# A matmul with batch normalization: four output stores of the last column tile issued as two transfers each

## The chip, the cores and the metric

The kernel runs on one core of a Trainium2 chip. The metric is the device time of one execution in microseconds (us), median of three runs. Details are read from one further execution, taken with the hardware profiler.

## The reference

```python
x: (16, 512, 1024) float32, weight: (1024, 768) float32, gamma = 1, beta = 0, eps = 1e-5
y = np.matmul(x, weight)
mean = np.mean(y, axis=(0, 1), keepdims=True)
var = np.var(y, axis=(0, 1), keepdims=True)
y_norm = (y - mean) / np.sqrt(var + eps)
return (gamma * y_norm + beta).astype(np.float32)
```

Mean and variance are taken for each of the 768 columns over all 8192 rows, so no value of a column can be written before all rows of that column are multiplied.

## The kernel before, in words

The 8192 rows are C = 16 chunks of CH = 512 rows, the 768 columns NT = 6 tiles of P = 128. GpSimd's queue loads x and the weight from HBM and casts them to bf16 on the way; VectorE transposes x in blocks of 32, and TensorE multiplies. The first two column tiles are computed with rows on the partitions, the other four with columns on the partitions; these have to be turned back before they are stored. Statistics are gathered by VectorE, ScalarE and GpSimd beside the matmuls. A column tile is finished, normalized and stored while TensorE works on the next one. What is left at the end is the last column tile (nt = 5).

The functions do not emit instructions at once. Each makes a `task` with a due time, engines, dependencies and buffers, and `arrange` puts all tasks into one order from estimated durations. The tasks then emit in that order, and `seq` (line 293) chains every instruction to the one before it on its engine, so that each engine, SyncE (SP) with its store queue too, works strictly in the order planned.

The part around the change is the loop over `ends` (lines 1363 to 1396). It cuts the last column tile into eleven blocks of rows, in the order of their first chunk c: two of 256 rows, two of 512, six of 1024 (c = 3, 5, 7, 9, 11, 13) and one of 512 (c = 15). For each block:
- `norm_part` (line 1374, VectorE) scales and shifts the bf16 block `y_sb` with the final coefficients `fss`, which `affine` (line 1350) has made;
- `turn_block` (line 1069, TensorE) transposes it, 128 by 128 at a time, into a PSUM bank `o_ps`;
- `copy` (line 1387, ScalarE) copies the bank to the SBUF tile `o_sb` of 128 partitions, as float32;
- `store` (lines 1389 to 1392, SP's queue) writes it to the output `out_dram`. A partition holds `count` rows of 128 floats, 512 bytes each, that go to rows of the output which lie 128 rows apart. With 1024 rows in the block, a partition sends 8 pieces of 512 bytes, and the store carries 512 KB.

Stores ahead of these, from the ring buffer (lines 1208, 1228 and 1281), use the same queue of SP. The transfers of SP's queue take their completion semaphores in turn from a set of eight, so a transfer also waits for the landing of the eighth before it.

Of the kernel before, what the change touches and what calls it, by code (L numbers as in the profile page):

```python
# [227 lines left out]
def kernel(  # L228
# [9 lines left out]
    nc = tc.nc  # L238
# [9 lines left out]
    P = 128  # L248
# [27 lines left out]
    MODE = {2:'xact',3:'xact',4:('pe',)*8}  # L276
    MODE = {nt: m if isinstance(m, tuple) else (m,) * (C // GY) for nt, m in MODE.items()}
    RAW, RAWADD, RAWDUE = {2:(0,2),3:(0,),4:(0,2,4)}, {2:'POOL',3:'POOL',4:'POOL'}, {2:14.0,3:8.0,4:8.0}
    RING = 3 * CH // 32 * KQ // 2
    ENG = {"ACT": nc.scalar, "DVE": nc.vector, "POOL": nc.gpsimd, "SP": nc.sync}  # L280

    x_flat = x.flatten_outer_dims()
    out_flat = out.flatten_outer_dims()
# [9 lines left out]
    def seq(bi):  # L293

        ins = bi.ins
        prev = last.get(ins.engine)
        if prev is not None:
            tc.add_manual_dep(
                ins, prev,
                mybir.DependencyInfo(mybir.DependencyClass.NoSync, mybir.DependencyReason.DATA),  # L300
                reason="order",
            )
        last[ins.engine] = ins.name
        return bi
# [5 lines left out]
    ident = singles.tile([P, P], bf16)  # L310
    ring = singles.tile([P, RING], f32)
    w_sb = singles.tile([P, JW, 2, N], bf16)
# [42 lines left out]
    tasks, turns = [], {}  # L355
    banks, xts, ys, sqs, rings = Pool(8), Pool(XT), Pool(YB), Pool(SQ), Space(RING)

    def task(prio, engines, emit, deps=(), lock=False, **kw):
        t = Task(prio, engines, emit, deps, **kw)
        t.lock = lock  # L360
        tasks.append(t)
        return t

    def dve(occ):
        return {"DVE": (occ, occ + 0.09)}

    def act(occ):
        return {"ACT": (occ, occ + 0.11)}
# [81 lines left out]
    for kind, n, *n1 in order:  # L450
# [11 lines left out]
        m0 = n if kind == "p" else n * rows  # L462
        if m0 == M // 2:
            affine_loads = affine = task(t, {"SP": (5.0, 7.0)}, load_affine, [x_ready[m0 // CH - 3, 0, JW]])
        slot = Slot(rings, rows // 32 * KQ // 2)
# [9 lines left out]
        for i in range(rows // QR):  # L475
            c, q = divmod(m0 // QR + i, QPC)
# [9 lines left out]
        if rows % QR:  # L486
            t0 = rows // QR * QR // 32
            m1 = m0 + 32 * t0
            c, q = divmod(m1 // QR, QPC)
# [197 lines left out]
    def y_of(nt, c):  # L687
        return y_col.setdefault((nt, c // GY), Slot(ys))

    def y(nt, c, n=1):  # L690
        group = y_of(nt, c).y.rearrange("p g m -> p (g m)")
        return group[:, c % GY * CH:(c % GY + n) * CH]
# [259 lines left out]
    p0 = task(U, {"ACT": (0.6, 0.7), "DVE": (0.6, 0.7)}, keep_affine, dl, takes=[aff_slot])  # L952


    def rows_out(c, s0, s1, k):
        due = S + 5.0 + 0.62 * k
        n = s1 - s0
        slot = Slot(rings, n * NA)

        def norm(eng):  # L960
            slot.o = piece(slot).rearrange("p (s n) -> p s n", n=NA)
            seq(nc.vector.tensor_mul(  # L962
                slot.o, y_row[c].y[:, s0:s1], aff[0][:, None, :].to_broadcast([P, n, NA])))

        def add(eng):
            row = sum1[:, NA:2 * NA] if eng == "POOL" else aff[1]
            seq(ENG[eng].tensor_add(slot.o, slot.o, row[:, None, :].to_broadcast([P, n, NA])))  # L967

        def store(eng):
            m0 = c * CH  # L970
            seq(nc.sync.dma_start(
                out_flat[m0 + s0 * P:m0 + s1 * P, 0:NA].rearrange("(s p) n -> p s n", p=P), slot.o))

        keeps = [row_end[k][3] for k in row_end if k[0] == c]
        a = task(due, dve(0.3 * n), norm, [p0] + keeps, takes=[slot], uses=[y_row[c], aff_slot])
        b = task(due + 0.4, dve(0.3 * n) if k in ADDED else pool(0.59 * n), add, [a, p0] if k in ADDED else [a] + dl,
                 uses=[slot, aff_slot] if k in ADDED else [slot])
        task(due + 1.0, {"SP": (0.38, 0.4)}, store, [b], dma=n * NA * P * 4 / 1024 / 365.0 * 1.024,
             uses=[slot])
# [76 lines left out]
    def turn_block(prio, nt, m0, count, deps, uses):  # L1056

        bank = Slot(banks)
        todo = []

        def step():
            if not todo:
                o_ps = psum.tile([P, count, P], bf16, tag="b")
                bank.tile = o_ps
                for s in range(count):
                    c, i = divmod(m0 // P + s, RT)
                    todo.append((o_ps[:, s], y(nt, c)[:, i * P:(i + 1) * P]))
            dst, src = todo.pop(0)
            seq(nc.tensor.transpose(dst, src, ident))  # L1069

        def emit(eng):
            for _ in range(emit.task.count):
                step()

        emit.step = step
        t = task(prio, pe(0.0555 * count), emit, deps, takes=[bank], uses=uses)
        emit.task = t
        turns[t] = [count, count]
        return t, bank

    def ga_block(c, due):
# [36 lines left out]
        turns[t] = [RT * GA, RT * GA]  # L1118
        d = task(due, {"ACT": (0.905, 1.0), "DVE": (1.1, 1.2)}, copy, [t], takes=[slot], uses=[bank])
        task(due, {"SP": (0.38, 0.4)}, store, [d], dma=RT * NA * P * 4 / 1024 / 365.0 * 1.024, uses=[slot])  # L1120

    for c in range(RC, C):
# [69 lines left out]
    def raw_block(nt, c, due):  # L1192
        rslot, turned = raw[nt, c]
        bank, t, k, b_sb = raw_aff[nt]
        slot = Slot(rings, GY * RT * P)
        n = GY * RT

        def norm_raw(eng):
            slot.o = piece(slot).rearrange("p (s n) -> p s n", n=P)
            seq(nc.vector.tensor_mul(slot.o, rslot.r, bank.tile[:, None, 0:P].to_broadcast([P, n, P])))  # L1200

        def add_raw(eng):
            row = b_sb if eng == "POOL" else bank.tile[:, P:2 * P]
            seq(ENG[eng].tensor_add(slot.o, slot.o, row[:, None, :].to_broadcast([P, n, P])))  # L1204

        def store(eng):
            m0 = c * CH
            seq(nc.sync.dma_start(
                out_flat[m0:m0 + n * P, nt * P:(nt + 1) * P].rearrange("(s p) n -> p s n", p=P), slot.o))

        a = task(due, dve(1.18), norm_raw, [t, turned], takes=[slot], uses=[bank, rslot])
        on = RAWADD[nt]
        b = task(due + 0.4, dve(1.2) if on == "DVE" else pool(2.35), add_raw, [a, t if on == "DVE" else k],
                 uses=[slot] + ([bank] if on == "DVE" else []))
        task(due + 1.0, {"SP": (0.38, 0.4)}, store, [b], dma=n * P * P * 4 / 1024 * STORE * 1.024, uses=[slot])
# [103 lines left out]
    nt = NT - 1  # L1319
# [45 lines left out]
    for c, r0, rows in ends:  # L1365
        due = E + 2.0 + 0.6 * c
        n = max(rows // CH, 1)
        keeps = [col_end[nt, c + i][1] for i in range(n) if c + i < C - 1]
        keeps += [col_end[nt, C - 1, q][1] for q in range(len(PIECES))] if c + n == C else []
        norms = []  # L1370
        for i in range(n):
            def norm_part(eng, c=c + i, r0=r0, rows=min(rows, CH)):
                part = y(nt, c)[:, r0:r0 + rows]
                seq(nc.vector.tensor_scalar(  # L1374
                    part, part, fss[:, 0:1], fss[:, 1:2], op0=ALU.mult, op1=ALU.add))

            norms.append(task(due + 0.6 * i, dve(0.323 if rows >= CH else 0.26), norm_part, [af] + keeps,
                              uses=[y_of(nt, c + i)]))
        m0 = c * CH + r0
        count = rows // P  # L1380
        b, bank = turn_block(due + 0.6 * (n - 1), nt, m0, count, norms, [y_of(nt, c + i) for i in range(n)])
        slot = Slot(xts)

        def copy(eng, slot=slot, bank=bank, count=count):
            o_sb = xtpool.tile([P, count, P], f32, tag="xT")
            slot.o = o_sb
            seq(nc.scalar.copy(o_sb, bank.tile))  # L1387

        def store(eng, slot=slot, m0=m0, count=count):
            seq(nc.sync.dma_start(  # L1390
                out_flat[m0:m0 + count * P, nt * P:(nt + 1) * P].rearrange("(s p) n -> p s n", p=P),
                slot.o))

        d = task(due + 0.6 * (n - 1), act(0.05 + 0.107 * count), copy, [b], takes=[slot], uses=[bank])
        task(due + 0.6 * (n - 1), {"SP": (0.6, 0.6)}, store, [d], dma=count * P * P * 4 / 1024 * STORE * 1.024,
             uses=[slot])
# [41 lines left out]
```

## Time and profile before

| what | us |
|---|---|
| median of three runs | 207.98 (207.83 to 208.24) |
| the profiled execution, whole | 208.35 |
| its span, first to last instruction | 206.6 |
| TensorE busy in the span | 190.2 (92%) |
| VectorE, ScalarE, GpSimd busy | 161.5, 149.0, 121.5 |
| last copy into `o_sb` ends (line 1387) | 196.95 |
| last store of `o_sb` is issued (line 1390) | 200.5 |

The profile's page has the busy time of each engine, the span cut in 40 slices with the busy share in tenths, and the share and the GB/s of the 16 DMA engines. The chain of waits follows the work that ended last back in time. Windows give the same figures for stretches that one chooses. The DMA view lists the packets of each queue and the transfers by line, with their time from issue to landing. No view gives the number of the DMA engine that a packet ran on. SP's own instructions are not counted as busy; "SPq" marks what it issues. The DMA share can be above 1 because packets of one engine overlap.

### The profile page before, as it was taken

What the parts mean: (1) busy time and instruction counts of PE and PEld (TensorE: products, weight loads), DVE (VectorE), ACT (ScalarE), POOL (GpSimd) and SP (SyncE); (2) the same over time, 40 slices, a digit from 0 to 9 for tenths busy, and PEclk for the clock granted to TensorE, in tenths of its full rate; (3) what the DMA queues carried; (4) which work ended last, traced back from release to release, by engine and by line L of the source; (5) the groups of instructions that cost most, each with busy time, mean ns of one, the idle gap of its engine ahead of it and who ended that gap; (6) DMA issues with size and microseconds to landing.
All of it is one profiled execution on the core that took longest, in us unless ns stands there. A gap on an engine that the chain in (4) does not pass through costs nothing. (4 is left out here: it accounts for less than half of the span.)

```text
span 206.6 us, 3499 instructions
## 1 busy us (share of the span) xinstructions
PE 190.2 (92%) x1202; PEld 115.6 (56%) x1202; DVE 161.5 (78%) x255; ACT 149.0 (72%) x273; POOL 121.5 (59%) x143
## 2 busy tenths in 40 slices
PE   7999999999999999999999999999999999995700
PEld 3467555656588888776855444444444445463700
DVE  4031979989999899969989999879999995668500
ACT  2001461479989989999889968989997979758910
POOL 7776964786499989997202999466603302741000
PEclk9999999999999999999999999999999999999665
DMA  5999999999999999999498699998999998999996
GB/s 76 163 199 194 191 196 196 199 195 196 190 194 197 195 197 195 196 197 192 89 135 229 231 333 335 275 363 230 354 291 235 336 316 217 349 343 345 345 347 181
DMA packets 98562, 48.74 MB, mean 236 GB/s; under 512 B 24304, under 2 KB 98032, under 8 KB 98544
## 3 DMA queue, kind: packets, MB, share of 16 engines
q0 software_dynamic: 34624, 18.36, 64.7%
q1 hardware_dynamic: 63920, 30.16, 53.4%
q8 instruction: 9, 0.15, 0.3%
q14 instruction: 9, 0.07, 0.1%
HBM read 36.71 MB, written 25.17 MB: 300 GB/s over the span
## 5 line engine op out<-in xcount | busy, mean ns | idle before, releaser
L577 PEld LDWEIGHTS <-w_sb 128*128 128x128 bf16 x520 | 50.4, 97 | 58.2 <-issue 0.5
L577 PE MATMUL y_ps<-xT_sb,w_sb 128*128 128x512 bf16 (+1 forms) x272 | 59.5, 371 | 0.0
L577 PE MATMUL y_ps<-x_pl,w_sb 128*128 128x512 bf16 x248 | 57.1, 379 | 0.2 <-ACT y_sb L717 0.2
L405 POOL DMA_DIRECT2D ring<-in_x_dram x76 | 47.4, 627 | 11.4 <-DMA ring<-in_x_dram 4.0
L512 PE MATMUL y_ps<-w_sb,xT_sb 128*128 128x256 bf16 x448 | 50.6, 273 | 0.6 <-DMA ring<-in_x_dram 0.4
L512 PEld LDWEIGHTS <-xT_sb 128*128 128x128 bf16 x448 | 43.5, 98 | 8.3 <-DVE xT_sb L437 2.0
L437 DVE STREAM_TRANSPOSE xT_sb<-ring 128x1024 f32<-128x1024 f32 (+1 forms) x29 | 31.2, 1112 | 13.9 <-DMA ring<-in_x_dram 13.7
L967 POOL TENSOR_TENSOR ring<-ring,sum 128x1024 f32<-128x1024 f32 (+1 forms) x11 | 23.8, 2186 | 20.0 <-DVE ring L962 20.0
L713 DVE BATCH_NORM_STATS2 stats<-y_ps 128x6 f32<-128x512 f32 x46 | 30.0, 682 | 5.7 <-PE y_ps L577 5.7
L549 ACT COPY x_pl<-xT_sb 128x1024 bf16<-128x1024 bf16 x31 | 31.6, 1059 | 1.9 <-DVE xT_sb L437 1.7
L717 ACT CAST y_sb<-y_ps 128x512 bf16<-128x512 f32 x51 | 28.4, 593 | 4.8 <-DVE stats L713 3.1
L661 ACT ACTIVATE sq_sb<-y_ps 128x512 f32<-128x512 f32 x28 | 16.3, 609 | 17.5 <-PE y_ps L512 16.9
L668 POOL TENSOR_TENSOR sum<-sum,sq_sb 128x512 f32<-128x512 f32 x20 | 25.6, 1281 | 3.4 <-ACT sq_sb L661 2.8
L664 DVE TENSOR_TENSOR sum<-y_ps,sum 128x512 f32<-128x512 f32 x28 | 18.9, 675 | 6.3 <-ACT sq_sb L661 5.3
L674 ACT CAST y_sb<-y_ps 128x512 bf16<-128x512 f32 x28 | 16.2, 597 | 8.1 <-DVE sum L664 7.8
L1204 POOL TENSOR_TENSOR ring<-ring,sum 128x1024 f32<-128x1024 f32 x6 | 14.4, 2424 | 10.5 <-issue 7.5
L962 DVE TENSOR_TENSOR ring<-y_sb,a_ps 128x1024 f32<-128x1024 bf16 (+1 forms) x16 | 16.7, 1076 | 0.6 <-DMA out_dram<-ring 0.6
L1069 PE MATMUL o_ps<-ident,y_sb 128*128 128x128 bf16 x104 | 13.8, 248 | 2.5 <-DVE y_sb L1374 2.5
L430 DVE STREAM_TRANSPOSE xT_sb<-ring 128x2048 bf16<-128x2048 bf16 x6 | 13.5, 2289 | 0.3 <-DMA ring<-in_x_dram 0.2
L1258 ACT CAST ring<-ring 128x1024 f32<-128x1024 bf16 x13 | 13.4, 1051 | 0.0
L593 PE MATMUL idle_ps<-idle_sb 128*128 128x512 f32 x18 | 10.7, 753 | 1.5 <-DVE idle_sb L316 1.5
L1171 POOL COPY sum<-sum 32x64 f32<-32x64 f32 (+1 forms) x7 | 3.0, 433 | 15.3 <-ACT sum L1171 8.7
(105 smaller groups left out, 161.5 us busy)
## 6 DMA issues: line engine op xcount, KB each, us to landing
out_dram<-ring SPq DMA_DIRECT2D x37, 512.0 KB, 3.8
ring<-in_x_dram POOLq DMA_DIRECT2D x52, 256.0 KB, 8.8
out_dram<-o_sb SPq DMA_DIRECT2D x6, 512.0 KB, 6.0
ring<-in_x_dram POOLq DMA_DIRECT2D x16, 128.0 KB, 5.7
w_sb<-in_weight_dram POOLq DMA_DIRECT2D x8, 192.0 KB, 6.2
out_dram<-ring SPq DMA_DIRECT2D x6, 256.0 KB, 2.8
ring<-in_x_dram POOLq DMA_DIRECT2D x4, 192.0 KB, 7.7
out_dram<-o_sb SPq DMA_DIRECT2D x3, 256.0 KB, 4.2
```

The costliest lines, as they stand in the source:

```text
L405: bi = seq(nc.gpsimd.dma_start(x_bf[32 * i:32 * i + 32], src[:, :, KQ * i:KQ * (i + 1)]))
L437: seq(nc.vector.transpose(dst, src[:, :, jw0:jw1]))
L512: seq(nc.tensor.matmul(y_ps[:, s], x_of(c, jw, e, t * P, (t + 1) * P), w_sb[:, jw, e, 0:NA], start=(s == 0 and jw == 0 and e == 0), stop=( ...
L549: seq(nc.scalar.copy(dst, pairs) if eng == "ACT" else ENG[eng].tensor_copy(dst, pairs))
L577: seq(nc.tensor.matmul(y_ps, w_sb[:, jw, e, nt * P:(nt + 1) * P], moving(c, jw, e, q0 * QR, q1 * QR, parted), start=(jw == 0 and e == 0 an ...
L661: seq(nc.scalar.activation(sq_sb[:, 0:n], slot.tile[:, 0:n], AF.Square))
L664: seq(nc.vector.tensor_add(sum1, slot.tile[:, 0:n], sum1))
L668: seq(ENG[eng].tensor_add(acc, acc, state["sq"][:, 0:n]))
L713: seq(nc.vector.bn_stats(dst, slot.tile))
L717: seq(nc.scalar.copy(y(nt, c), slot.tile))
L962: seq(nc.vector.tensor_mul(slot.o, y_row[c].y[:, s0:s1], aff[0][:, None, :].to_broadcast([P, n, NA])))
L967: seq(ENG[eng].tensor_add(slot.o, slot.o, row[:, None, :].to_broadcast([P, n, NA])))
```

## The change

Four of the eleven stores of the last column tile, those of the blocks with c = 3, 5, 7 and 9, are issued as two transfers each: the first over the partitions below a cut, the second over the rest. The cuts are at 120, 126, 104 and 108 of 128 partitions. The second transfer follows the first directly on SP's queue. The other seven stores remain whole, as one transfer over 128 partitions. The estimated durations of the tasks are left as they were, and the order on PE, DVE, ACT and POOL is the same; SP issues four transfers more. The line of these issues is 1390 before and 1394 after.

```diff
     RAW, RAWADD, RAWDUE = {2:(0,2),3:(0,),4:(0,2,4)}, {2:'POOL',3:'POOL',4:'POOL'}, {2:14.0,3:8.0,4:8.0}
+    CUTS = {3: 120, 5: 126, 7: 104, 9: 108}
     RING = 3 * CH // 32 * KQ // 2
...
-        def store(eng, slot=slot, m0=m0, count=count):
-            seq(nc.sync.dma_start(
-                out_flat[m0:m0 + count * P, nt * P:(nt + 1) * P].rearrange("(s p) n -> p s n", p=P),
-                slot.o))
+        def store(eng, slot=slot, m0=m0, count=count, cut=CUTS.get(c, P)):
+            dst = out_flat[m0:m0 + count * P, nt * P:(nt + 1) * P].rearrange("(s p) n -> p s n", p=P)
+            for p0, p1 in ((0, cut), (cut, P)):
+                if p0 < p1:
+                    seq(nc.sync.dma_start(dst[p0:p1], slot.o[p0:p1]))
```

SP's queue at the end, as transfers of partitions x rows x 128 floats, after the change:

```
L1394 DMACopy out_dram<-o_sb 128x2x128 x2
L1394 DMACopy out_dram<-o_sb 128x4x128 x2
L1394 DMACopy out_dram<-o_sb 120x8x128
L1394 DMACopy out_dram<-o_sb 8x8x128
L1394 DMACopy out_dram<-o_sb 126x8x128
L1394 DMACopy out_dram<-o_sb 2x8x128
L1394 DMACopy out_dram<-o_sb 104x8x128
L1394 DMACopy out_dram<-o_sb 24x8x128
L1394 DMACopy out_dram<-o_sb 108x8x128
L1394 DMACopy out_dram<-o_sb 20x8x128
L1394 DMACopy out_dram<-o_sb 128x8x128 x2
L1394 DMACopy out_dram<-o_sb 128x4x128
```

## The prediction

> **What bounds the kernel now.** First the page's slices of the whole span, to see which resource is full at the end.
>
> ```profile
> PE   7999999999999999999999999999999999995700
> DVE  4031979989999899969989999879999995668500
> ACT  2001461479989989999889968989997979758910
> DMA  5999999999999999999498699998999998999996
> ```
>
> One digit is 5.2 us. In the last two slices PE, DVE and ACT are idle and the DMA row still reads 9 and 6: the kernel ends on stores. Second, the chain of waits, whose last pieces are these.
>
> ```profile
> 189.89 5.66 ACT o_sb L1387 x7
> 195.55 0.92 ACTq L1433
> 196.46 0.49 ACT o_sb L1387
> ```
>
> The last copy into o_sb ends at 196.95 us and the span at 206.6, so 9.6 us lie behind all computing. Third, the windows of the tail, which tell what those 9.6 us are made of (columns: window, its length, busy time of PE, PEld, DVE, ACT and POOL, PE clock, DMA share, GB/s).
>
> ```profile
> 199.00:203.00 4.00, 0.00 (x0) 0.00 (x0) 0.00 (x0) 0.00 (x0) 0.00 (x0) 0.50 1.15 347
> 203.50:204.00 0.50, 0.00 (x0) 0.00 (x0) 0.00 (x0) 0.00 (x0) 0.00 (x0) 0.50 1.06 317
> 204.00:204.20 0.20, 0.00 (x0) 0.00 (x0) 0.00 (x0) 0.00 (x0) 0.00 (x0) 0.50 0.31 92
> 204.20:204.40 0.20, 0.00 (x0) 0.00 (x0) 0.00 (x0) 0.00 (x0) 0.00 (x0) 0.50 0.20 59
> 204.40:204.70 0.30, 0.00 (x0) 0.00 (x0) 0.00 (x0) 0.00 (x0) 0.00 (x0) 0.50 0.11 32
> 204.70:205.10 0.40, 0.00 (x0) 0.00 (x0) 0.00 (x0) 0.00 (x0) 0.00 (x0) 0.50 0.07 22
> 205.40:206.60 1.20, 0.00 (x0) 0.00 (x0) 0.00 (x0) 0.00 (x0) 0.00 (x0) 0.50 0.00 0
> ```
>
> All 16 DMA engines together move 347 GB/s, so one moves 347/16 = 21.7. In 204.70:205.10 the rate is 22: a single engine is left, and alone it runs at the pace that it had beside fifteen others. The engines are therefore limited one by one, and bytes shifted between them cost and gain time one for one. By the same division 92 GB/s is about four engines, 59 two to three, 32 one and a half. Read that way, twelve engines end by about 204.05 us, two at about 204.3, one at about 204.55 and the last at about 205.3. Call them the on-time engines and the late ones (0.35, 0.35, 0.6 and 1.4 us behind the earliest, which end at 203.9). From 205.3 the closing takes 1.3 us.
>
> Where the lateness comes from is in the DMA view of two short windows, 180.3 to 181.5 and 185.6 to 186.2: among the store packets lies a packet of the instruction queues.
>
> ```profile
> q8 instruction: 1, 0.02, 5.0%
> q14 instruction: 1, 0.01, 3.2%
> ```
>
> 5.0% of 16 engines over 1.2 us is 0.96 us of one engine, 3.2% over 0.6 us is 0.31 us. Two more of the small kind lie in 178.9:179.5 and 186.8:187.4. Four fetches on four engines and four late engines: I take the one for the other (an estimate from these rows).
>
> **The unit of the sum.** A 512 KB store takes 524288 B / 347 GB/s = 1.51 us, in which each engine moves 8 partitions of 8 rows of 512 B. One partition more or less on an engine is 1.51/8 = 0.189 us.
>
> **What the change moves.** No engine's instructions move but SP's, which issues 15 transfers on line 1394 where it issued 11 on line 1390. Bytes, rows of 512 B and copies stay. What is open is on which engines the cut transfers run. The trace has only transfers of 128 or 32 partitions, both multiples of 16, each in equal shares on all 16 engines. So I bound it: at one end a cut transfer is still spread evenly by packets and nothing moves; at the other it keeps equal shares of whole partitions and runs on as many engines as divide its partition count, always the same first ones. The numbers chosen, 15x8, 14x9, 13x8 and 12x9, lie nearer to the second end, since equal whole shares are what every row shows, and I take it. [...]
>
> Per engine, in partitions, before 8 for each of the four stores, 32 in all; after:
> - 120 and 8: 8 each on engines 0 to 14, and 1 each on 0 to 7.
> - 126 and 2: 9 each on 0 to 13, and 1 each on 0 and 1.
> - 104 and 24: 8 each on 0 to 12, and 2 each on 0 to 11.
> - 108 and 20: 9 each on 0 to 11, and 2 each on 0 to 9.
>
> The sums are 40 for engines 0 and 1, 39 for 2 to 7, 38 for 8 and 9, 36 for 10 and 11, then 25, 17, 8 and 0 for 12 to 15. So twelve engines gain 4 to 8 partitions (0.76 to 1.51 us) and four lose 7, 15, 24 and 32 (1.3, 2.8, 4.5 and 6.0 us). The lateness to be cured is at most 1.4 us, and a balance of all 16 would need only 7 partitions off the latest; the cut takes far more than that off the four and puts it on the rest.
>
> **The sum.** An on-time engine of 0 or 1 ends at 203.9 to 204.05 plus 1.51, that is 205.4 to 205.55, already past the old end of 205.3. Four more completion packets on each engine (the DMA view of 188 to 203 us counts 208 packets under 512 B for 13 transfers, 16 each) cost at most a 512 B packet's time, 512/21.7 = 24 ns each, 0.1 us in all; I take 0.04. Late engines that are among the loaded ones end later: the one at 204.55, on 2 to 7, at 204.55 + 1.32 + 0.04 = 205.9; one at 204.3 there at 205.65. For which engines are late no view gives numbers. In the packet records the engines restart in one order after the idle time at 172 us, and the latest one is about the 14th in it, the others about the 2nd, 7th and 9th; if that is the order of their numbers, the latest is spared and the others are not. That is what I take: the end of the DMA goes from 205.3 to 205.9, 0.6 us later. The profiled execution took 208.35 us, 206.6 of span and 1.75 around it, and becomes 208.95; the median of the three runs is 207.98, so 208.6.
>
> **What is hidden.** SP spends 0.42 us on a store's issue when nothing holds it (shortest of the row) and 1.35 in the median.
>
> ```profile
> L1390 SPq DMA_DIRECT2D out_dram<-o_sb x11: 419/1348/1617, 189.8 to 200.5; - x11
> DMA to landing us min/median/max: 3.8/5.1/6.1
> ```
>
> Four more issues are 4 x 0.42 = 1.7 us of SP time, with only further stores queued behind them. They lie beside transfers that land 3.8 to 6.1 us after their issue, so the engines have that much queued; without this cover the end would move by up to 1.7 us. Each transfer also waits for the landing of the eighth before it. For the last store that is now the 126-partition transfer, landing about 41 x 0.189 = 7.7 us before the end, near 198.2, when an engine has some 7 us of work in front of the last store. The spared engines run dry meanwhile, but 20 partitions of the last three stores take them 3.8 us; they are done near 201.5.
>
> **The rivals.**
> - *The latest engine is among the loaded ones.* Then the end is 205.3 plus 0.76 to 1.55: 208.8 to 209.5. For it: four spared engines of sixteen hold a given one by chance one time in four. Against it: its place in the order of restart.
> - *All late engines are spared.* Then engines 0 and 1 set the end, 205.45 to 205.6: 208.1 to 208.3.
> - *It ends faster: the transfers on fewer engines do not always run on the same ones.* If the first engine moves on from transfer to transfer, the skipped shares fall on different engines and the added ones spread. The latest loses 8 partitions once (1.5 us) and no on-time engine takes more than 3 (0.57): the DMA ends near 204.7, which gives 207.4. It decides as soon as the latest is skipped and no on-time engine takes over 4 partitions more (204.05 + 0.76 = 204.8). For it: 0.35 to 1.4 us of lateness is there to be won, mean lateness only 0.2. Against it: nothing in the trace shows a moving start.
> - *The cut transfers run slower.* Engines of an uneven cut may meet at the same part of SBUF. The nearest row is the loads of 32 partitions each, 195 GB/s on the page's slices against 347 here, though those also read HBM at twice what they write. At that pace a store takes 2.69 us, and four lose up to 4.7; a third of it, 1.5, is as much as I would give: 209.5 to 211. [...]
> - *The cut moves nothing between engines.* Even spreading by packets leaves the end at 205.3 plus 0.04: 208.0.
>
> **How the numbers follow.** About 0.2%, or 0.42 us, is what a measurement of this kernel can tell from no change. Chances: forecast (208.2 to 208.9, likeliest 208.6) 0.36; latest engine loaded 0.19; all late ones spared 0.13; slower transfers 0.09; nothing moved 0.06; faster 0.17. Slower: 0.19, 0.09 and all but 0.05 of the forecast, 0.59. Same: 0.13, 0.06 and that 0.05, 0.24. Faster: 0.17. The range from 207.4 to 209.7 leaves out half of the faster case and most of the slower transfers, some 0.16.
>
> **What would show it.** In the windows of the tail after, the rate should leave 347 GB/s well before 203 us as the spared engines run out (15, 14, 13 and 12 engines at work are 325, 304, 282 and 260 GB/s), stay near 260 until about 205, and drop to two or three engines near 205.5. A rate that holds 347 to 203.5 says that nothing was moved; an end of DMA before 204.9 says that the faster rival holds; single-engine rates below 21.7 say that the transfers slow each other. The prediction is wrong at its root if engines 0 and 1 don't get 8 partitions more.

## The result, and the profile after

The changed kernel is slower: 211.23 us in the median of four runs (210.23 to 211.91) against 208.06 for the kernel before on the same chip; ratio 1.0149, 95% interval 1.0106 to 1.0192, that is 3.1 us more (2.2 to 4.0). The profiled execution took 211.42 us, with a span of 209.6. The forecast was 208.6, the range ended at 209.7.

Computing is over at the same moment as before. This is the end of the chain of waits, after:

```profile
190.06 5.66 ACT o_sb L1388 x7
195.72 0.92 ACTq L1435
196.63 0.49 ACT o_sb L1388
```

The last copy ends at 197.1 us, 0.2 later than before; the rest lies behind it, nearly all of it in the stores. The windows of the tail, after (columns as in the prediction: the last two are DMA share and GB/s):

```profile
192.00:194.00 2.00, 2.00 (x21) 2.00 (x20) 2.00 (x7) 2.00 (x4) 0.00 (x0) 0.50 1.15 344
196.00:198.00 2.00, 0.00 (x0) 0.00 (x0) 0.00 (x0) 1.12 (x2) 0.00 (x0) 0.97 0.88 252
198.00:200.00 2.00, 0.00 (x0) 0.00 (x0) 0.00 (x0) 0.00 (x0) 0.00 (x0) 0.50 0.83 235
200.00:202.00 2.00, 0.00 (x0) 0.00 (x0) 0.00 (x0) 0.00 (x0) 0.00 (x0) 0.50 0.75 214
202.00:204.00 2.00, 0.00 (x0) 0.00 (x0) 0.00 (x0) 0.00 (x0) 0.00 (x0) 0.50 0.96 284
204.00:206.00 2.00, 0.00 (x0) 0.00 (x0) 0.00 (x0) 0.00 (x0) 0.00 (x0) 0.50 1.06 321
206.00:207.00 1.00, 0.00 (x0) 0.00 (x0) 0.00 (x0) 0.00 (x0) 0.00 (x0) 0.50 0.84 252
207.00:208.00 1.00, 0.00 (x0) 0.00 (x0) 0.00 (x0) 0.00 (x0) 0.00 (x0) 0.50 0.14 41
```

The rate leaves 347 GB/s when the first cut store reaches the engines and falls to 214. Twelve engines at 21.7 would still move 260, so more is lost than the work of the spared four. It returns near the end, and the last engine stops at 208.1 instead of 205.3. SP's stores of o_sb answer to the row of line 1390 before:

```profile
L1394 SPq DMA_DIRECT2D out_dram<-o_sb x15: 419/772/1810, 190.0 to 203.8; - x15
```

The last store is issued at 203.8 instead of 200.5.

A smaller term moved too, one that the sum held fixed: the closing, from the last DMA packet to the end of the span. It takes 1.50 us after and 1.25 before. At the end SP waits for the eight completion semaphores one after another, in the same order in both traces, 0.06 us each. With 11 transfers the last one to land has the last semaphore of that order; with 15, four waits follow it, 0.24 us. The other traces agree: 1.24 to 1.25 us with 11 transfers, 1.68 to 1.69 with 12, 1.56 with 14, 1.48 to 1.51 with 15, 1.31 to 1.33 with 18.

The hardware queue of SP, from the page after:

```profile
q1 hardware_dynamic: 63942, 30.16, 52.6%
```

Before it had 63920 packets for the same 30.16 MB. The 22 more are all under 512 B (24326 on the page after, 24304 before). Counted as completion packets, one for each engine that a transfer runs on, they are 15+8+14+2+13+12+12+10 = 86 against 4 x 16 = 64. So by this count each cut transfer runs on as many engines as divide its partitions, as the prediction took it. The same count fits the runs below: +64 with four cuts at 112 or 64, +28 at 120, 0 at 126, +36 at 104, +24 at 108, +32 at 117.

### The profile page after: what moved, and what is told of

Same layout as the page of the kernel before. It is cut to its first block, busy times and chain, and to the rows that moved or that the text cites. A ratio compares the mean times of both kernels' runs of the same rounds, so it can differ in the third digit from the quotient of the medians.

```text
span 209.6 us, 3489 instructions
## 1 busy us (share of the span) xinstructions
PE 189.4 (90%) x1188; PEld 115.5 (55%) x1202; DVE 161.4 (77%) x255; ACT 148.9 (71%) x273; POOL 121.5 (58%) x143
## 2 busy tenths in 40 slices
DMA packets 98584, 48.74 MB, mean 232 GB/s; under 512 B 24326, under 2 KB 98054, under 8 KB 98566
## 3 DMA queue, kind: packets, MB, share of 16 engines
q1 hardware_dynamic: 63942, 30.16, 52.6%
## 5 line engine op out<-in xcount | busy, mean ns | idle before, releaser
L578 PE MATMUL y_ps<-xT_sb,w_sb 128*128 128x512 bf16 (+1 forms) x264 | 58.7, 371 | 0.5
```

The lines of the kernel that those rows point to most:

```text
L578: seq(nc.tensor.matmul(y_ps, w_sb[:, jw, e, nt * P:(nt + 1) * P], moving(c, jw, e, q0 * QR, q1 * QR, parted), start=(jw == 0 and e == 0 an ...
```

## The experiments

All differences are against the kernel before on the same chip, as ratios with their 95% interval; 0.001 is 0.21 us. Every run with 15 transfers has 0.24 us of longer closing in its difference. "Stretch" is the length of a packet's record, worked out from a window as DMA share x 16 engines x 512 B / rate; undisturbed it is 1.15 x 16 x 512 / 347 GB/s = 27.1 ns. Edits are to the changed kernel and shown in short. What is said of single packets or engines comes from the packet records of the traces, which give each packet's start, length and size, but not its engine.

**Cuts that move no load, and a cut along the rows.**

```diff
-    CUTS = {3: 120, 5: 126, 7: 104, 9: 108}
+    CUTS = {3: 112, 5: 112, 7: 112, 9: 112}    # all112
+    CUTS = {3: 64, 5: 64, 7: 64, 9: 64}        # all64
```

> All four cuts at 112 of 128 partitions (112 and 16, both multiples of 16, so 7 and 1 partitions on each of 16 engines). Load theory (time goes where partitions are added, 0.189 us each): no engine gets more, so 0.0 +- 0.2 us against the kernel before, tail at 347 GB/s to 203.5 us. Slow-transfer theory (a transfer not over all 128 partitions moves slower because engines meet in SBUF): up to about 1.6 us slower, the part of the change's 3.2 us that 8 partitions (1.5 us) don't explain, with the rate below 347 while the cut stores move. Issue theory (more transfers hold SP back): up to 1.7 us slower, with the rate at 347 and then dry engines.

> All four cuts at 64 of 128 partitions (4 and 4 partitions on each of 16 engines): no load is moved. Load theory: 0.0 +- 0.2 us. Slow-transfer theory: the strongest case, since each transfer reads one half of SBUF's partitions only; a rate clearly under 347 GB/s during the four stores, 1 to 6 us slower. Issue theory: as with 112 and 16, up to 1.7 us.

Measured: all112 1.0024 (1.0009 to 1.0040), 0.5 us; all64 1.0052 (1.0027 to 1.0077), 1.1 us. The windows of the two, all112 first:

```profile
196.00:201.00 5.00, 0.00 (x0) 0.00 (x0) 0.00 (x0) 0.87 (x2) 0.00 (x0) 0.64 0.97 275
```

```profile
194.00:203.00 9.00, 0.20 (x4) 0.03 (x1) 0.00 (x0) 3.29 (x5) 0.00 (x0) 0.77 0.95 270
```

Load alone is refuted: every engine has its 32 partitions, yet the rate is 275 and 270 for 347, and packets are 28.9 and 28.8 ns long. The packets are 6 to 7% longer, which is far from the missing fifth; the share, 0.97 and 0.95 for 1.15, says that engines also stand idle.

```diff
-            for p0, p1 in ((0, cut), (cut, P)):
-                if p0 < p1:
-                    seq(nc.sync.dma_start(dst[p0:p1], slot.o[p0:p1]))
+            for s0, s1 in ((0, count // 2), (count // 2, count)) if cut < P else ((0, count),):
+                seq(nc.sync.dma_start(dst[:, s0:s1], slot.o[:, s0:s1]))    # rows44
```

> The same four stores as two transfers each, but cut along the rows of a partition: each transfer has all 128 partitions with 4 of their 8 rows, 256 KB. Slow-transfer theory (what is slow is a transfer that doesn't span all 128 partitions): no change, 0.0 +- 0.3 us, 347 GB/s to 203.5 us. Issue theory (the number of transfers): as slow as the cuts at 64 and 64, +1.1 to +1.5 us. Load theory: 0.0.

Measured: 1.0003 (0.9985 to 1.0020). Its window:

```profile
194.00:202.00 8.00, 0.50 (x9) 0.33 (x6) 0.00 (x0) 2.59 (x4) 0.00 (x0) 0.69 1.15 346
```

As many transfers as in all64, of the same size, and the rate stays at 346. The number of transfers and SP's issues cost nothing that shows in the rate, and the 0.24 us of closing lies within the interval; what costs in all64, with 270 GB/s, goes with transfers that don't hold all 128 partitions. Nor do the engines of all64 lack issued work: at the end of each issue of its cut stores 1310 to 1470 packets are issued and not done, for 1440 to 1580 in rows44, some 80 for an engine on the average.

**Four equal cuts that move load.**

```diff
+    CUTS = {3: 120, 5: 120, 7: 120, 9: 120}    # all120; all126, all104, all108, all117 alike
```

> All four cuts at 120 of 128 partitions: 8 partitions an engine on the first 15, then 1 each on the first 8; 36 on engines 0 to 7, 32 on 8 to 14, 0 on 15, against 32. Load theory: on-time engines end 0.75 us later (204.8); the latest ends at 203.9 if it is engine 15, at 205.3 if among 8 to 14, at 206.05 if among 0 to 7: -0.5, 0.0 or +0.75 us. Slow-transfer theory: 1.6 us or more on top.

> All four cuts at 126: 9 partitions on each of 14 engines, then 1 each on the first 2; 40 on engines 0 and 1, 36 on 2 to 13, 0 on 14 and 15. Load theory: on-time engines 2 to 13 end 0.75 us later, 0 and 1 1.5 us later (205.5), a late one among 2 to 13 up to 0.75 after 205.3: +0.2 to +0.8 us. Slow-transfer theory: in addition what the transfer itself loses, 0.8 us as with 120 and 8 or more, since shares of 9 partitions fit no regular pattern: +1.0 to +2.5 us.

> All four cuts at 104 of 128 partitions: 8 an engine on the first 13, then 2 each on the first 12; 40 on engines 0 to 11, 32 on 12, 0 on 13 to 15. Load theory: 8 more, +1.5 us for loaded engines; with the latest among them +1.5 us in the time, without it +0.5 to +0.8. Slow-transfer theory: another 1.6 us or more on top.

> All four cuts at 108: 9 partitions on each of 12 engines, then 2 each on the first 10; 44 on engines 0 to 9, 36 on 10 and 11, 0 on 12 to 15. The run with 72 in the last store puts the latest engine among the first 9. Load theory: 12 partitions more, +2.3 us. Slow-transfer theory on top: 0.5 to 1 us as in the runs with four equal cuts, 2.8 to 3.3 us in all. If the four pairs of the change simply add up, this run has to be far slower than that (four times 3.2 less the other three, some 7 us).

> All four cuts at 117: 9 partitions on each of 13 engines, then 1 each on the first 11, so 40 on engines 0 to 10, as in the run with 104 (40 on 0 to 11), but in shares of 9 instead of 8. Load theory alone: as slow as that run (2.3 us). Neighbour theory (shares of 8 put engines 4 apart on partitions 32 apart at the same moment, and those wait for each other; shares of 9 don't): the load only, +1.5 us, with packets unstretched while the long transfers run.

(The statement that the latest engine is among the first 9 is a misreading of mine, told below.) Measured, with the added partitions of the most loaded engines and the window between 195 and 202 us:

| run | partitions of a share | added, us by load | ratio | us | GB/s, stretch |
|---|---|---|---|---|---|
| all126 | 9 | 8 on 2 engines, 4 on 12: 1.5, 0.75 | 1.0043 (1.0022 to 1.0063) | 0.9 | 294, 27.3 ns |
| all117 | 9 | 8 on 11: 1.5 | 1.0070 (1.0045 to 1.0095) | 1.5 | 274, 27.5 ns |
| all108 | 9 | 12 on 10: 2.3 | 1.0129 (1.0102 to 1.0157) | 2.7 | 252, 27.3 ns |
| all120 | 8 | 4 on 8: 0.75 | 1.0076 (1.0048 to 1.0103) | 1.6 | 242, 29.5 ns |
| all104 | 8 | 8 on 12: 1.5 | 1.0109 (1.0068 to 1.0150) | 2.3 | 232, 29.0 ns |

The windows, in the order of the table:

```profile
196.00:201.00 5.00, 0.00 (x0) 0.00 (x0) 0.00 (x0) 1.66 (x3) 0.00 (x0) 0.74 0.98 294
```

```profile
196.00:202.00 6.00, 0.00 (x0) 0.00 (x0) 0.00 (x0) 1.51 (x3) 0.00 (x0) 0.70 0.92 274
```

```profile
195.00:201.00 6.00, 0.00 (x0) 0.00 (x0) 0.00 (x0) 2.23 (x3) 0.00 (x0) 0.78 0.84 252
```

```profile
196.00:202.00 6.00, 0.00 (x0) 0.00 (x0) 0.00 (x0) 1.68 (x3) 0.00 (x0) 0.74 0.87 242
```

```profile
196.00:202.00 6.00, 0.00 (x0) 0.00 (x0) 0.00 (x0) 1.62 (x3) 0.00 (x0) 0.77 0.82 232
```

With shares of 9 the rate is that of the engines at work (14, 13 and 12 of them make 304, 282 and 260 GB/s), packets keep their length (27.3 to 27.5 ns for 27.1), and the time is near what the added load gives. With shares of 8 the rate is well under it (15 and 13 engines would make 325 and 282), packets are stretched (29.5 and 29.0 ns), and some 0.8 us come on top of the load. The cleanest pair is all104 against all117: both have 13 engines at work and 40 partitions on the most loaded, 232 against 274 GB/s; the intervals of their times still overlap. In all108 the load is seen on one engine: the one that ends last takes 9 and 2 partitions of every pair, by the times of its completion packets, and ends 17.80 us after the first store of o_sb is issued, for 15.52 before. These 2.28 us are its 12 partitions more. The neighbour theory in the expectation of all117 takes it that each engine gets neighbouring partitions in the order of the engines, which no view shows. The packet lengths agree with it, 29.0 and 29.5 ns with shares of 8 against 27.3 to 27.5 with shares of 9; the next run, shares of 8 alone at 27.7 ns, doesn't, so it isn't shown to be the cause.

**First transfers alone.**

```diff
-            for p0, p1 in ((0, cut), (cut, P)):
+            for p0, p1 in ((0, cut),):    # first120 with all cuts at 120; firsts with the cuts of the change
```

> Cuts at 120 as in the run with all four at 120, but the second transfers, over the last 8 partitions, are left out, and with them 4 x 32 KB of the output. Engines 0 to 14 get 8 partitions as before, engine 15 none; eleven transfers as before. Load theory: not slower; 0.0, or up to 0.75 us faster if the latest engine is the 15th. Slow-transfer theory: the transfer over 120 partitions is itself slow, about +0.5 to +0.8 us. Issue theory: 0.0.

> The change with its four second transfers left out (and 8, 2, 24 and 20 partitions of four blocks of the output with them): 8, 9, 8 and 9 partitions on the first engines, 34 for 32. Load theory: +0.38 us. What the second transfers add by load (6 of the first engine's 8 partitions, 1.1 us) must be gone; what is left above 0.4 us is what the uneven first transfers lose by themselves, 0.1 each by the run with 120 only: +0.4 to +0.8 us.

Measured: first120 0.9984 (0.9968 to 1.0001), firsts 1.0058 (1.0035 to 1.0082), 1.2 us. Shares of 8 by themselves, all alike, lose next to nothing: 316 GB/s between 194 and 202 us where 15 engines make 325, stretch 27.7 ns. Against the expectation of 0.5 to 0.8 this fell. The four first transfers of the change, 8, 9, 8 and 9 partitions in turn, lose 0.8 us more than their load of 0.38. So shares of 8 lost time where small second transfers (all120, all104) or shares of 9 (firsts) lie between them, and none that shows in first120; why a regular row of them comes through isn't settled.

**One store as eight transfers of 16 partitions.**

```diff
+            for a in range(8):    # c = 5 only
+                seq(nc.sync.dma_start(dst[16*a:16*a+16], slot.o[16*a:16*a+16]))    # eightC
+                seq(nc.sync.dma_start(dst[a::8], slot.o[a::8]))                    # eightS
+                seq(nc.sync.dma_start(dst[a::8], slot.o[16*a:16*a+16]))            # eightP
```

> One store only (c = 5) as eight transfers of 16 neighbouring partitions each (0 to 15, 16 to 31, ...), 1 partition on each of 16 engines a time; no load is moved. SBUF theory (engines that read neighbouring partitions at one moment wait for each other; each of the four transfers of 16 neighbours in the run with cuts at 112 cost about 0.1 to 0.2 us): 8 x 0.1 to 0.4, +0.8 to +3 us, with a rate well under 347 GB/s for some 2 us. Load theory: 0.0. Should SP's issues limit (8 x 0.4 us for 1.5 us of engine time), the rate falls too, but equally in the next two runs.

> The same eight transfers, but each takes every eighth partition (a, a+8, ... a+120) and so every eighth of the rows in HBM; same bytes, same 1 partition an engine. SBUF theory: clearly less lost than with neighbours, half or under. HBM theory (the engines wait for each other where they write neighbouring rows): also less. Issue theory: the same loss as with neighbours.

> Eight transfers of 16 neighbouring partitions as in the first of the three, written to every eighth row as in the second, so that the output's rows of this one block are in another order. SBUF theory: as slow as the first. HBM theory: as fast as the second. Issue theory: all three alike.

Measured: eightC 1.0023 (1.0010 to 1.0035), eightS 1.0086 (1.0061 to 1.0112), eightP 1.0032 (1.0022 to 1.0042). That is 0.5, 1.8 and 0.7 us, against what was expected of the first two. The times don't tell the theories apart, since SP's issues limit at least eightC and eightS, and eightS the most. SP's issues of eightC, then of eightS:

```profile
L1394 SPq DMA_DIRECT2D out_dram<-o_sb x8: 323/431/1034, 194.5 to 198.6; - x8
```

```profile
L1394 SPq DMA_DIRECT2D out_dram<-o_sb x8: 591/598/1100, 193.4 to 198.4; - x8
```

A transfer over every eighth partition takes 0.60 us to issue, one over neighbours 0.43, and 64 KB in 0.60 us is 109 GB/s, in 0.43 us 152; the windows have 112 and 159. The packets do tell. Windows of eightC, eightS and eightP while these transfers run:

```profile
197.50:199.50 2.00, 0.00 (x0) 0.00 (x0) 0.00 (x0) 1.14 (x2) 0.00 (x0) 1.00 0.71 159
```

```profile
197.00:199.50 2.50, 0.00 (x0) 0.00 (x0) 0.00 (x0) 0.49 (x1) 0.00 (x0) 1.00 0.41 112
```

```profile
196.00:198.00 2.00, 0.00 (x0) 0.00 (x0) 0.00 (x0) 1.25 (x2) 0.00 (x0) 0.67 0.73 168
```

Stretch is 36.6, 30.0 and 35.6 ns. With neighbours in SBUF it is large in either order of the rows in HBM (36.6 and 35.6), and smaller with every eighth partition (30.0). eightS has fewer packets in flight, but that isn't the reason: where 10 to 14 are in flight at a packet's start, its record is 32 to 39 ns long on the average in eightC, 33 to 37 in eightP and 28 to 29 in eightS. That puts the longer packets of eightC and eightP down to which partitions are read in SBUF, not to the order of the rows in HBM.

**Where the latest engine is.**

```diff
+    CUTS = {15: 104}    # last104
+    CUTS = {15: 72}     # last72
```

> No cut but one, in the last store (c = 15, 4 rows a partition, 256 KB), at 104 of 128: engines 0 to 12 keep their 8 partitions (0.094 us each at 4 rows), 0 to 11 get 2 more (+0.19 us), 13 to 15 none (-0.75 us). Load theory with the latest engine among 13 to 15: the DMA ends at about 204.75 instead of 205.3, 0.5 us faster; with the latest among 0 to 11: 205.5, 0.2 us slower. Slow-transfer theory: little on top, a quarter of a 512 KB pair's loss at most, 0.1 to 0.2 us, since little is queued behind.

> One cut in the last store (c = 15, 0.094 us a partition) at 72: 8 partitions each on engines 0 to 8, then 56 as 4 each on engines 0 to 13. Engines 0 to 8 get 4 more (+0.375 us), 9 to 13 get 4 less, 14 and 15 none. The run with 104 there ended as if the latest engine were among the first 12. Load theory: if it is among 9 to 11, the DMA ends 0.38 us earlier, near 204.95; if among 0 to 8, 0.38 us later, near 205.7. The time moves by the same, near what can be measured; the trace decides.

Measured: last104 1.0013 (0.9995 to 1.0031), last72 1.0016 (1.0003 to 1.0029); no gain. In the packet records the engine that ends last gets both parts of the store cut at 104, the second 0.19 us long, and ends 15.72 us after the first store of o_sb is issued, for 15.52 before: the 0.19 that two more partitions of 4 rows cost. So it is among the 12 that take both parts in this trace. My expectation for 72 was wrong in itself: by the queue's count the first part runs on 12 engines, not 9 (10 packets more, 12 + 14 - 16). The 12 engines get 6 + 4 = 10 partitions, the same 0.19 us, and the last one ends 15.70 us after that issue. So this run says no more than last104: among the 12 that take both parts. That it is among the first 9, as two expectations have it, isn't shown.

The other traces don't agree, and the latest engine can be followed in them: in each, one engine ends the fourth store of o_sb 5.67 to 5.69 us after the first store's issue, over 0.5 us behind all others. In all108 it takes part in every pair, as said above. In all126 no completion packet lies where nine more partitions would end for it (7.38 us; none from 6.63 to 7.64), so it has no share of the first cut store. In only9, below, it ends c = 7 at 10.20 and c = 11 at 11.72, one whole store later, so c = 9 gave it nothing. The latest engine is not the same one from trace to trace, and last104 doesn't tell which it is in the change. In both traces of the change it takes 8 of the first 120 partitions, so it isn't the one that this transfer spares; more isn't settled.

**The change in parts, and once more.**

```diff
+    CUTS = {9: 108}                     # only9
+    CUTS = {3: 120, 5: 126, 7: 104}     # without9
```

> The change's last cut alone (c = 9 at 108 and 20). Load theory: 3 partitions more, +0.57 us. Slow-transfer theory: 0.1 to 0.25 on top, +0.7 to +0.8 us. If the pair at 108 is what makes the change's 3.2 us, +1.5 us or more.

> The change without its cut of c = 9: 29 partitions for 24 on engines 0 and 1, 28 on 2 to 7, 27 on 8 and 9. Load theory: +0.57 to +0.94 us; slow-transfer theory: with 0.1 to 0.25 a pair, +0.9 to +1.7 us. If the pairs add up with the run of c = 9 alone, the two make 3.2 us.

> The changed kernel once more, for a narrower interval and for a second trace beside the run with 117: load (latest engine among the first 9, 6 to 8 partitions more) 1.1 to 1.5 us, and 1.5 us or more of slow packets on top, +2.6 to +3.4 us. If the first measurement was off, about +1.9, the mean of the four runs with equal cuts.

Measured: only9 1.0048 (1.0029 to 1.0066), 1.0 us; without9 1.0060 (1.0040 to 1.0081), 1.25 us; the change again 1.0109 (1.0082 to 1.0137), 2.3 us. The parts make 2.25 us, as much as the second measurement, so no pair carries the loss alone. That is a sum of medians; the traces don't bear out that the losses add up: from the first store's issue to the end of DMA it is 15.50 us in only9 and 15.98 in without9, for 15.52 before, and their closing is 0.43 and 0.31 us longer. The second measurement lies at the low end of the first one's interval. From the first store's issue to the end of DMA it is 18.2 us in the first trace of the change and 16.6 in the second; the 1.1 us of the second are no more than load alone may give. The rate falls in the second trace as well:

```profile
198.00:200.00 2.00, 0.00 (x0) 0.00 (x0) 0.00 (x0) 0.11 (x1) 0.00 (x0) 0.87 0.81 228
200.00:202.00 2.00, 0.00 (x0) 0.00 (x0) 0.00 (x0) 0.00 (x0) 0.00 (x0) 0.50 0.83 243
```

So the loss is 2.3 to 3.1 us, and the time of a single trace isn't to be taken for it.

## Why the prediction was wrong

- *The kernel ends on stores, each engine limited by itself.* Right. In all108 twelve engines move 252 GB/s, 21 each, and the engine that ends last is later by the time of its 12 added partitions. Moving bytes onto engines that are already at work costs their time, as forecast, and the sign was right.
- *How the cut transfers are shared out.* Right as to the number of engines, by the count of completion packets in every run it is given for (22 more after, 28 in all120, 36 in all104). That they are always the same first ones was my assumption: no run shows the numbers of the engines, and so not the 4 to 8 partitions that the sum gives to each of engines 0 to 11. What shows is that in all108 one engine, the one that ends last, takes part in all four pairs.
- *Which engines are late.* This step had nothing to stand on. I took the place in the order of restart for an engine's number, and so the latest engine for a spared one. The traces have it among the loaded ones in last104, last72 and all108 and without a share of a cut store in all126 and only9. Where it is loaded, the sum has to carry its own 4 to 8 partitions, 0.76 to 1.51 us instead of 0.6, which was the rival "the latest engine is among the loaded ones". Which of the two holds in the change stays open; load is at most 1.51 us.
- *That cut transfers run at full pace.* The step that failed. The forecast put this term at nothing, and its rival, 209.5 to 211 us, at 0.09. The windows after show 214 to 252 GB/s where 260 was forecast to hold. With no load moved it costs 0.8 us in all64, closing aside, and nothing in rows44, whose transfers have all 128 partitions. In the change it is what is left: 2.3 to 3.1 us, less at most 1.51 of load and 0.24 of closing, leave at least 0.5 to 1.3 us. The second measurement's interval alone, 1.7 to 2.9 us, wouldn't exclude that nothing is left; the rates under 260 GB/s in both traces do. Load alone, at its most, would have been 207.98 + 1.51 = 209.5 us, inside the range of up to 209.7.
- *The closing.* Taken as fixed at 1.3 us; four more transfers made it 0.24 us longer.
- *What is hidden.* SP's four more issues cost nothing by themselves but the closing: rows44 has as many and loses nothing that can be measured. SP's last issue 3.3 us later I read as a consequence of slow engines: from the first cut store on, 1079 packets or more are always issued and not done when SP begins an issue, some 90 for each of twelve engines on the average. No run tests this by itself.
- *The faster rival.* Refuted: no run gained. A moving first engine isn't seen: through the four pairs of all108 the rate stays at that of twelve engines, and the engine that ends last takes part in all four.

What isn't settled: how the change's loss is split between load and slow transfers, what engines do in the idle part of their time in all112 and all64, for which the profile has no record, and why equal shares of 8 without second transfers (first120) come through.

## What to carry to other kernels

When a tail is bound by DMA engines that are each at their pace, a gain by balance is at most the lateness of the latest engine less the mean lateness (1.4 less 0.2 us here), and must be sized in the unit of one partition (0.19 us) before transfers are cut; first find out which engine is late, and in more than one trace. Count the transfers, too: what follows the last landing changed with their number, by up to 0.43 us. Four stores cut along their rows, with all 128 partitions in each transfer, cost nothing that could be measured here (rows44, 1.0003, 0.9985 to 1.0020); cut along partitions, even into equal loads, they cost 0.5 us (all112) and 1.1 us (all64). The completion packets in the queue's count (22 more after) told for free on how many engines the cut transfers run.

## What the runs showed of the hardware that was not expected

- Two transfers over 64 partitions each, 4 on every engine, moved 270 GB/s (all64) where one over 128 moved 347; shares of 9 partitions on 12 to 14 engines kept 97% of those engines' full rate (274 of 282, 252 of 260, 294 of 304), shares of 8 with small second transfers 74 to 82% (242 of 325, 232 of 282).
- A transfer of 16 partitions with a step of 8 took SP 0.60 us to issue (median of eightS), one of 16 neighbours 0.43 (eightC).
- Packets of the instruction queues, of 0.31 us (three) and 0.96 us (one) in the kernel before, lie among the stores, each on a single DMA engine, and the lateness that is seen beside them stays until the end: in the kernel before, the latest engine is 1.4 us behind the earliest at the fourth store of o_sb and 1.4 at the last, each store giving every engine the same share.
- The closing of this kernel takes 1.25 to 1.69 us, by how many of SP's eight semaphores are waited for behind the last landing, 0.06 us each in the traces before and after.
